# Modulation tiles multiplied in pairs, and the Hyena filters' two directions on the two halves of the array rows

## The chip, the core and the metric

The kernel runs on one NeuronCore of a Trainium2 chip. The metric is the device time of one execution in microseconds; a comparison is made between medians of runs on the same chip. One core has TensorE (PE; its weight loads are shown as PEld), VectorE (DVE), ScalarE (ACT), GpSimd (POOL) and SyncE (SP), which here only issues transfers, and 16 DMA engines. TensorE has two clock levels, 1.2 and 2.4 GHz; the profile shows the granted one as a share of the higher.

## What is computed

One inference step of a two-layer hybrid backbone, for a prompt of 128 tokens and a latent grid of 128 tokens with shared weights, in fp32. The parts that matter here:

```python
mod = silu(c) @ w_mod[l] + b_mod[l]          # 2048 -> 6 x 2048, for c_ctx and c; w_mod[l] is 100 MB
sh1, sc1, g1, sh2, sc2, g2 = split(mod, 6)
h = rms_norm(x, ln_mix) * (1 + sc1) + sh1
u_hy, u_gla, u_mla = split(h @ w_in)         # three mixers read the same h
x = x + g1 * (concat(hyena(u_hy), gla(u_gla), mla(u_mla)) @ w_out)
h = rms_norm(x, ln_ffn) * (1 + sc2) + sh2
x = x + g2 * ((silu(gate) * up) @ w_ffn_out) # gate, up = split(h @ w_ffn_in)

# hyena filters, the same for both token groups, once per layer
h = sin(freq[0] * (z @ w1 + b1))             # z: 128 x 33, w1: 33 x 64
h = sin(freq[1] * (h @ w2 + b2))             # w2: 64 x 64
k = (h @ w3) * decay                         # w3: 64 x (2 directions x 2 orders x 512 channels)
```

## The kernel before, in words

Both token groups lie side by side as 256 columns. The large products (`gemm_steps`, matmuls on line 343, tiles `pg`) split weights and activations into a high and a low fp32r part and run three matmuls for each block; for each k tile `weights` loads a tile `w` (five buffers), ScalarE writes `wh`, VectorE writes `wl`.

The modulation of a layer has six parts of 2048 columns. For layer 0 the first two are made in the prologue by `mod_first` (line 207, tiles of 256 columns and six buffers). Of the others, some run on VectorE beside the feed-forward part (`mod_dve`), and five run on TensorE (`mod_pe`, line 242): parts 2, 4 and 3 of layer 0 and parts 3 and 4 of layer 1, beside the three mixers and the output projection. For one part, `mod_pe` goes over 16 k tiles of 128 x 2048 fp32 (1 MB each, tag `mw` of the pool `mp`, which has **two** buffers). Each tile takes four matmuls: the stationary operand is the 128 x 32 piece `sc` of the conditioning vectors, the moving one a 128 x 512 view of the tile, and the four write the four 32-row strips of one PSUM bank `mps`, so they sit side by side in the four column groups of the array. A plain fp32 matmul stands in the profile as two records, so one tile is eight records of line 242.

`mod_pe` is a generator. `mod_tick(w)` moves it on by `rate` x w steps: `gemm_steps` ticks once for each k tile (weight: columns / 1024), `mla` with weight 10 for each pair of heads, `gla` and `hyena` with weight 14 for each token group; the rate is 0.36 in layer 0 and 0.2 in layer 1. So a tick of 14 in layer 0 is five steps with nothing else written between them. A step of the old form loads the next tile and multiplies the one loaded before.

The order on each engine is not the order of the code: the framework's scheduler places an instruction when its inputs are ready by its own reckoning, earlier code first. `add_manual_dep(a, b, no_sync)` keeps a behind b in that order. All weight loads and modulation loads are issued by SP, in order, and a load whose buffer is still in use holds back those behind it. The xs, constants, rows and filter weights are issued from ACT's queue.

`hyena_filters(pool, l)` runs in the prologue of layer 0 for both layers, between the first gemms: two small layers with a sine (lines 558 to 572), then for each of two orders and two directions one matmul with 64 rows of contraction (line 580) times `decay`, and the transform matrices (lines 585 to 589). The results go to DRAM and are read back by `hyena`. The bias and frequency rows come in through `rows2`, which line 516 transposes into `v2T`.

Of the kernel before, what the change touches and what calls it, by code (L numbers as in the profile page):

```python
# [17 lines left out]
KT = D // 128  # L18
# [9 lines left out]


MSTEP = 3  # L30
AHEAD = 4
FQ = 1
SPLIT = (4, 4, 4, 4)
# [69 lines left out]
def tile_backbone(ctx, tc, T, O):  # L103
# [52 lines left out]
            table["users"].append(r.ins.name)  # L156
        return r

    mm = nc.tensor.matmul

    def px(shape):
        return ps_x.tile(shape, F32, tag="x", name="px")
# [26 lines left out]
    def quads(w):  # L189
        return w.rearrange("p (k q j) -> p q k j", q=4, j=32)  # L190
# [39 lines left out]
    def mod_load(l, m, kt, pool):  # L230
        w = pool.tile([128, D], F32, tag="mw", name="mw")
        nc.sync.dma_start(w, T["w_mod"][l, kt * 128:(kt + 1) * 128, m * D:(m + 1) * D])
        return w

    def mod_pe(l, m, pool):
        ps = ps_m.tile([128, 512], F32, tag="mod", name="mps")
        nxt = mod_load(l, m, 0, pool)
        for kt in range(KT):
            w, nxt = nxt, mod_load(l, m, kt + 1, pool) if kt + 1 < KT else None
            wv = quads(w)  # L240
            for q in range(4):
                mm(ps[32 * q:32 * q + 32, :], sc[:, kt], wv[:, q], start=(kt == 0), stop=(kt == KT - 1))  # L242
            yield
        mod_finish(l, m, ps)
        yield

# [219 lines left out]
    with PR("px0") as pool:  # L466
        rows = pool.tile([128, 128], F32, name="rows")
        nc.sync.dma_start(rows[0:16], r128(T["c_ctx"], 16))
        nc.sync.dma_start(rows[16:32], r128(T["c"][0], 16))
        nc.scalar.dma_start(ident, T["mats"][:, 0])  # L470
        p = px([128, 128])
        nc.tensor.transpose(p[:, :32], rows[:32, :], ident[:32, :32])
        nc.vector.memset(sc, 0.0)
        act(sc[:, :, 0:2], p[:, 0:32].rearrange("p (g k) -> p k g", g=2), AF.Silu)

        at = 32
        for nm in ("ln_mix", "ln_ffn"):
            for l in range(DEPTH):
                nc.scalar.dma_start(rows[at:at + 16], r128(T[nm][l], 16))
                at += 16  # L480
        nc.scalar.dma_start(rows[at:at + 16], r128(T["ln_final"], 16))
        at += 16
        for nm, n in (("mla_q_norm", 3), ("mla_kv_norm", 2), ("gla_norm", 1)):
            for l in range(DEPTH):
                nc.scalar.dma_start(rows[at:at + n], r128(T[nm][l], n))
                at += n
        p = px([128, 128])
        nc.tensor.transpose(p[:, :at], rows[:at, :], ident[:at, :at])
        nc.vector.tensor_copy(out=vT[:, 32:at], in_=p[:, 32:at])

        for l in range(DEPTH):
            rb = pool.tile([128, 128], F32, tag="rb", name="rb")[:96]
            nc.scalar.dma_start(rb, r128(T["b_mod"][l], 96))
            p = px([128, 96])
            nc.tensor.transpose(p, rb, ident[:96, :96])
            nc.vector.tensor_copy(out=bT[:, l].rearrange("p m k -> p (m k)"), in_=p)

        for _ in mod_first(0, SPLIT[0], mp0, AHEAD):
            pass

        rows2 = pool.tile([128, 128], F32, tag="rb", name="rows2")
        nc.vector.memset(rows2, 0.0)
        at = 0
        for l in range(DEPTH):
            nc.scalar.dma_start(rows2[at:at + 36], T["hy_conv_w"][l].rearrange("i (r c) -> (i r) c", c=128))
            at += 36
        for l in range(DEPTH):
            nc.scalar.dma_start(rows2[at:at + 12], r128(T["hy_conv_b"][l], 12))
            at += 12
        for l in range(DEPTH):  # L510
            nc.scalar.dma_start(rows2[at:at + 1, :64], T["hy_filt_b1"][l:l + 1])
            nc.scalar.dma_start(rows2[at + 1:at + 2, :64], T["hy_filt_b2"][l:l + 1])
            nc.scalar.dma_start(rows2[at + 2:at + 4, :64], T["hy_filt_freq"][l])
            at += 4
        p = px([128, 128])
        nc.tensor.transpose(p[:, :at], rows2[:at, :], ident[:at, :at])
        nc.vector.tensor_copy(out=v2T, in_=p[:, :at])

        for half in range(2):
            xs = []  # L520
            for nm in ("x_prompt", "x_sample"):
                xt = pool.tile([128, D // 2], F32, tag="xin", name="xin", bufs=4)
                nc.scalar.dma_start(xt, T[nm][0, :, half * 1024:half * 1024 + 1024])
                xs.append(xt)
            for k4 in range(2):
                for g in range(2):
                    p = px([128, 4, 128])
                    for j in range(4):
                        k = 4 * k4 + j
                        nc.tensor.transpose(p[:, j], xs[g][:, 128 * k:128 * k + 128], ident)  # L530
                    k = 8 * half + 4 * k4
                    dst = xT[:, k:k + 4, 128 * g:128 * g + 128]
                    if g:
                        act(dst, p)
                    else:
                        nc.vector.tensor_copy(out=dst, in_=p)
        ss = SquareSum(pool)
        for k in range(0, KT, 2):
            ss.add(k, on_pe=(k == KT - 2), last=(k == KT - 2))
        rsq(rstd, ss.ps, ss.acc[:, 0:256])  # L540


    def hyena_filters(pool, l):
        w1 = pool.tile([33, 64], F32, tag="fw1", name="fw1")
        w2 = pool.tile([64, 64], F32, tag="fw2", name="fw2")
        zt = pool.tile([33, 128], F32, tag="fzt", name="fzt")
        skip = pool.tile([1, 1024], F32, tag="fsk", name="fsk")
        dec = pool.tile([128, HC], F32, tag="fdec", name="fdec")
        nc.scalar.dma_start(zt, T["zt"])
        nc.scalar.dma_start(w1, T["hy_filt_w1"][l])  # L550
        nc.scalar.dma_start(w2, T["hy_filt_w2"][l])
        nc.scalar.dma_start(dec, T["decay"])
        nc.scalar.dma_start(skip, T["hy_skip"][l:l + 1].rearrange("a o c -> a (o c)"))
        col = V2_F + 4 * l
        src, wgt = zt, w1
        for i in range(2):
            p = px([64, 128])
            mm(p, wgt, src, start=True, stop=True)
            b, f = v2T[:64, col + i:col + i + 1], v2T[:64, col + 2 + i:col + 3 + i]
            y = pool.tile([64, 128], F32, tag="fy", name="fy", bufs=2)  # L560
            k = pool.tile([64, 128], F32, tag="fk", name="fk")
            r = pool.tile([64, 128], F32, tag="fr", name="fr")
            ts(y, p, b, ALU.add, f, ALU.mult)
            ts(k, y, 1.0 / (2 * PI), ALU.mult)
            ts(k, k, 12582912.0, ALU.add)
            ts(k, k, 12582912.0, ALU.subtract)
            stt(r, k, -6.28125, y, ALU.mult, ALU.add)
            stt(r, k, -0.0019350051879882812, r, ALU.mult, ALU.add)
            stt(r, k, -3.019915981956753e-07, r, ALU.mult, ALU.add)
            ts(r, r, -3.1415925, ALU.max, 3.1415925, ALU.min)  # L570
            act(y, r, AF.Sin)
            src, wgt = y, w2
        for o in range(2):
            kt = {}
            for d in range(2):
                p = px([128, HC])
                c0 = (2 * d + o) * HC
                w3 = pool.tile([64, HC], F32, tag="fw3", name="fw3", bufs=2)
                nc.scalar.dma_start(w3, T["hy_filt_w3"][l, :, c0:c0 + HC])
                mm(p, src, w3, start=True, stop=True)  # L580
                kt[d, o] = pool.tile([128, HC], F32, tag=f"fkt{d}", name="fkt")
                tt(kt[d, o], p, dec, ALU.mult)
            tt(kt[0, o][0:1], kt[0, o][0:1], skip[:, o * HC:(o + 1) * HC], ALU.add)
            pr = px([128, HC])
            mm(pr, mats[:, M_FC], kt[0, o], start=True, stop=False)
            mm(pr, mats[:, M_BC], kt[1, o], start=False, stop=True)
            pi = px([128, HC])
            mm(pi, mats[:, M_FS], kt[0, o], start=True, stop=False)
            mm(pi, mats[:, M_BS], kt[1, o], start=False, stop=True)
            ks = pool.tile([128, 3, HC], F32, tag="fks", name="fks")  # L590
            act(ks[:, 0], pr)
            act(ks[:, 2], pr)
            nc.vector.tensor_copy(out=ks[:, 1], in_=pi)
            nc.vector.tensor_copy(out=ks[0:1, 2], in_=pi[0:1])
            nc.vector.memset(ks[0:1, 1], 0.0)
            nc.sync.dma_start(kspec[l][:, o], ks)
# [616 lines left out]
```

## Time and profile before

| what | value |
|---|---|
| median of 3 runs | 2512.07 us (2506.38 to 2512.3) |
| the profiled execution | 2512.27 us, its span 2510.5 us |
| PE busy | 2445.6 us (97%) |
| DVE busy | 1693.8 us (67%) |
| ACT busy | 1032.3 us (41%) |
| mean DMA rate | 239 GB/s, 601.21 MB |
| mean granted TensorE clock | 0.993 |

Times in rows are microseconds from the start of the span. A row of the timeline has start, length, engine, line, operation, output<-inputs, shape and the number of records merged in it; in brackets stands how long the engine had been idle before it, and what ended that. TensorE's matmuls are pipelined: the length of one is longer than the distance to the next, so what one costs is read from the distances between starts. A row of a table by stretches has the stretch, its length, the busy time (and number of records) of PE, PEld, DVE, ACT and POOL, the granted clock, the busy share of the DMA engines and GB/s. In a list of waits: waiter <- what it waited for, total us, times, longest. SPq and ACTq rows are transfers being issued.

### The profile page before, as it was taken

Reading aid. Unit: us, or ns where it says so; the run is one execution under the profiler, and the core shown is the slowest. Engines: PE = TensorE matmul, PEld = TensorE weight load, DVE = VectorE, ACT = ScalarE, POOL = GpSimd, SP = SyncE. Lnnn points to the kernel's source line nnn. Section 1 sums busy time; section 2 is a strip of 40 time slices with the busy share of each in tenths; the row PEclk is TensorE's granted clock in tenths of the full one; section 3 lists DMA queues with packets and bytes.
Section 4 is the critical chain, followed back from the end, with each engine's and each line's share of the span. In section 5 each row is a group of like instructions: output and inputs, shape, how many; then the busy total and the mean of one; then the engine's idle time right before and its main releaser. Section 6 shows DMA issues by size and latency. Waiting matters only on the chain.

```text
span 2510.5 us, 47020 instructions
## 1 busy us (share of the span) xinstructions
PE 2445.6 (97%) x19621; PEld 2254.7 (90%) x19621; DVE 1693.8 (67%) x2399; ACT 1032.3 (41%) x1405; POOL 0.2 (0%) x4
## 2 busy tenths in 40 slices
PE   6999999999999999999999999999999999999998
PEld 3567777999999999999998887899999999999998
DVE  2665555887879968988878556588684545454455
ACT  2334342454433333434446444335444334433443
POOL 0000000000000000000000000000000000000000
PEclk9999999999999999999999999999999999999998
DMA  8988888767768768777866667686765566555662
GB/s 291 332 297 306 292 298 301 282 221 250 264 224 292 284 228 302 238 258 258 288 227 190 214 240 243 218 298 215 252 234 178 184 185 185 177 186 166 184 204 93
DMA packets 167305, 601.21 MB, mean 239 GB/s; under 512 B 18576, under 2 KB 24882, under 8 KB 146612
## 3 DMA queue, kind: packets, MB, share of 16 engines
q1 hardware_dynamic: 164104, 592.27, 70.4%
q10 hardware_dynamic: 2988, 5.93, 0.7%
q8 instruction: 154, 2.52, 0.4%
q14 instruction: 59, 0.48, 0.1%
HBM read 592.03 MB, written 6.09 MB: 238 GB/s over the span
## 4 chain that ended last, share of the span: by engine, by line
PE 92%; DMA 4%; DVE 2%; ACT 1%; issue 0%; SPq 0%; DVEq 0%; ACTq 0%
PE pg L343 80%; DMA mw<-in_w_mod_dram 4%; PE mps L242 3%; PE px L862 2%; PE mps L207 1%; PE px L922 0%; PE px L426 0%; DVE macc L259 0%; PE px L268 0%; PE px L580 0%; PE px L623 0%; PE px L767 0%; DVE wl L126 0%; PE px L625 0%; PE px L914 0%
## 5 line engine op out<-in xcount | busy, mean ns | idle before, releaser
L126 DVE TENSOR_TENSOR wl<-w,wh 128x1024 fp32r<-128x1024 f32 (+3 forms) x816 | 872.2, 1086 | 547.5 <-ACT wh L153 543.2
L153 ACT ACTIVATE wh<-w 128x1024 fp32r<-128x1024 f32 (+3 forms) x816 | 767.8, 950 | 1140.3 <-PE pg L343 971.0
L343 PE MATMUL pg<-hh,wh 128*128 128x256 f32 x3648 | 1038.8, 286 | 9.9 <-ACT hh L153 9.1
L343 PE MATMUL pg<-hl,wh 128*128 128x256 f32 x3648 | 1035.0, 284 | 0.0
L343 PE MATMUL pg<-hh,wl 128*128 128x256 f32 x3648 | 1032.0, 284 | 2.7 <-DVE wl L126 2.7
L343 PEld LDWEIGHTS pg<-hh,wh 128*128 128x128 f32 x3648 | 688.8, 189 | 46.3 <-issue 26.5
L343 PEld LDWEIGHTS pg<-hl,wh 128*128 128x128 f32 x3648 | 691.4, 190 | 10.6 <-issue 9.1
L343 PEld LDWEIGHTS pg<-hh,wl 128*128 128x128 f32 x3648 | 689.8, 189 | 11.8 <-issue 7.2
L343 PE MATMUL pg<-al,wh 128*128 128x256 f32 x1408 | 396.8, 282 | 0.0
L343 PE MATMUL pg<-ah,wl 128*128 128x256 f32 x1408 | 395.0, 281 | 0.0
L343 PE MATMUL pg<-ah,wh 128*128 128x256 f32 x1408 | 395.0, 282 | 0.0
L259 DVE SCALAR_TENSOR_TENSOR macc<-mw,sc,macc 128x1024 f32<-128x1024 f32 x300 | 370.8, 1280 | 6.6 <-DMA mw<-in_w_mod_dram 6.6
L343 PEld LDWEIGHTS pg<-ah,wh 128*128 128x128 f32 x1408 | 264.6, 188 | 1.7 <-issue 1.7
L343 PEld LDWEIGHTS pg<-ah,wl 128*128 128x128 f32 x1408 | 265.6, 189 | 0.1
L343 PEld LDWEIGHTS pg<-al,wh 128*128 128x128 f32 x1408 | 265.5, 189 | 0.1
L242 PE MATMUL mps<-mw,sc 128*32 128x512 f32 x640 | 88.8, 604 | 10.4 <-DMA mw<-in_w_mod_dram 10.4
L131 DVE SCALAR_TENSOR_TENSOR xT<-pg,modv,xT 128x128 f32<-128x128 f32 x256 | 69.6, 343 | 24.0 <-PE pg L343 24.0
L343 PE MATMUL pg<-ymh,wh 128*128 128x256 f32 x256 | 72.4, 286 | 0.6 <-DVE xT L131 0.6
L343 PE MATMUL pg<-yml,wh 128*128 128x256 f32 x256 | 72.2, 283 | 0.0
L343 PE MATMUL pg<-ymh,wl 128*128 128x256 f32 x256 | 71.6, 283 | 0.0
L207 PE MATMUL mps<-mw,sc 128*32 128x256 f32 x512 | 45.2, 441 | 14.1 <-DMA mw<-in_w_mod_dram 14.1
L343 PEld LDWEIGHTS pg<-ymh,wh 128*128 128x128 f32 x256 | 48.8, 192 | 5.3 <-issue 5.0
(299 smaller groups left out, 1879.2 us busy)
## 6 DMA issues: line engine op xcount, KB each, us to landing
mw<-in_w_mod_dram SPq DMA_DIRECT2D x160, 1024.0 KB
w<-in_w_ffn_in_dram SPq DMA_DIRECT2D x256, 512.0 KB
w<-in_w_ffn_out_dram SPq DMA_DIRECT2D x176, 512.0 KB
w<-in_w_ffn_in_dram SPq DMA_DIRECT2D x128, 384.0 KB
mw<-in_w_mod_dram SPq DMA_DIRECT2D x64, 512.0 KB
w<-in_w_in_dram SPq DMA_DIRECT2D x64, 512.0 KB
w<-in_w_out_dram SPq DMA_DIRECT2D x64, 512.0 KB
w<-in_w_in_dram SPq DMA_DIRECT2D x64, 256.0 KB
```

The source lines that it names most:

```text
L126: r = nc.vector.tensor_tensor(out=out, in0=a, in1=b, op=op)
L131: r = nc.vector.scalar_tensor_tensor(out=out, in0=a, scalar=s, in1=b, op0=op0, op1=op1)
L153: r = nc.scalar.activation(out=out, in_=a, func=func, **k)
L207: mm(ps[32 * q:32 * q + 32, :], sc[:, kt], wv[:, q], start=(kt == 0), stop=(kt == KT - 1))
L242: mm(ps[32 * q:32 * q + 32, :], sc[:, kt], wv[:, q], start=(kt == 0), stop=(kt == KT - 1))
L259: r = nc.vector.scalar_tensor_tensor(out=acc[:, i, cs], in0=w[:, cs], scalar=c, in1=acc[:, i, cs], op0=ALU.mult, op1=ALU.add)
L343: mm(o, lt, rh, start=(ti == 0 and i == 0 and j == 0), stop=(ti == nt - 1 and i == len(ps) - 1 and j == 2))
L862: mm(o, a, b, start=(st and i == 0 and j == 0), stop=(en and i == len(steps) - 1 and j == 2))
```

## The change

1. `mod_pe` takes its tiles two at a time. One step loads both tiles of a pair, the next multiplies both, eight matmuls in a row, the tile loaded second first. `start` is now on tile 1 and `stop` on tile 14. The number of buffers stays two.
2. After such a pair the next `BURST` = 24 matmuls of the code that go through `mm` are tied behind the pair's last one, in order only. (Because `mm` is now a function, those matmuls all show line 164.)
3. In `hyena_filters` w1 and w2 are loaded twice side by side, so that the two sine layers give the same 64 rows twice, in partitions 0 to 63 and 64 to 127. The weights of the two directions lie in the two halves of one tile, and their two matmuls, each of 64 rows, are written one behind the other, into two PSUM banks.
4. For that, the bias and frequency rows are loaded twice into `rows2`.

```diff
+BURST = 24
...
-    mm = nc.tensor.matmul
+    burst = {"last": None, "left": 0}
+
+    def mm(*args, **kw):
+
+        r = nc.tensor.matmul(*args, **kw)
+        if burst["left"]:
+            burst["left"] -= 1
+            tc.add_manual_dep(r.ins, burst["last"], no_sync, reason="order")
+        return r
...
     def mod_pe(l, m, pool):
         ps = ps_m.tile([128, 512], F32, tag="mod", name="mps")
-        nxt = mod_load(l, m, 0, pool)
-        for kt in range(KT):
-            w, nxt = nxt, mod_load(l, m, kt + 1, pool) if kt + 1 < KT else None
-            wv = quads(w)
-            for q in range(4):
-                mm(ps[32 * q:32 * q + 32, :], sc[:, kt], wv[:, q], start=(kt == 0), stop=(kt == KT - 1))
+        for k0 in range(0, KT, 2):
+            ws = [mod_load(l, m, kt, pool) for kt in (k0, k0 + 1)]
             yield
+            burst["left"] = 0
+            for kt, w in ((k0 + 1, ws[1]), (k0, ws[0])):
+                wv = quads(w)
+                for q in range(4):
+                    r = mm(ps[32 * q:32 * q + 32, :], sc[:, kt], wv[:, q], start=(kt == 1), stop=(kt == KT - 2))
+            burst.update(last=r.ins.name, left=BURST)
+            if k0 + 2 < KT:
+                yield
         mod_finish(l, m, ps)
         yield
...
         for l in range(DEPTH):
-            nc.scalar.dma_start(rows2[at:at + 1, :64], T["hy_filt_b1"][l:l + 1])
-            nc.scalar.dma_start(rows2[at + 1:at + 2, :64], T["hy_filt_b2"][l:l + 1])
-            nc.scalar.dma_start(rows2[at + 2:at + 4, :64], T["hy_filt_freq"][l])
+            for h in (slice(0, 64), slice(64, 128)):
+                nc.scalar.dma_start(rows2[at:at + 1, h], T["hy_filt_b1"][l:l + 1])
+                nc.scalar.dma_start(rows2[at + 1:at + 2, h], T["hy_filt_b2"][l:l + 1])
+                nc.scalar.dma_start(rows2[at + 2:at + 4, h], T["hy_filt_freq"][l])
...
-        nc.scalar.dma_start(w1, T["hy_filt_w1"][l])
-        nc.scalar.dma_start(w2, T["hy_filt_w2"][l])
+        for i in range(2):
+            nc.scalar.dma_start(w1[:, i], T["hy_filt_w1"][l])
+            nc.scalar.dma_start(w2[:, i], T["hy_filt_w2"][l])
...
-            p = px([64, 128])
-            mm(p, wgt, src, start=True, stop=True)
+            p = px([128, 128])
+            mm(p, wgt.rearrange("p a c -> p (a c)"), src[0:wgt.shape[0]], start=True, stop=True)
...
+            w3 = pool.tile([128, HC], F32, tag="fw3", name="fw3", bufs=2)
             for d in range(2):
-                p = px([128, HC])
                 c0 = (2 * d + o) * HC
-                w3 = pool.tile([64, HC], F32, tag="fw3", name="fw3", bufs=2)
-                nc.scalar.dma_start(w3, T["hy_filt_w3"][l, :, c0:c0 + HC])
-                mm(p, src, w3, start=True, stop=True)
+                nc.scalar.dma_start(w3[64 * d:64 * d + 64], T["hy_filt_w3"][l, :, c0:c0 + HC])
+            ps = [px([128, HC]) for _ in range(2)]
+            for d in range(2):
+                r = slice(64 * d, 64 * d + 64)
+                mm(ps[d], src[r], w3[r], start=True, stop=True)
+            for d in range(2):
                 kt[d, o] = pool.tile([128, HC], F32, tag=f"fkt{d}", name="fkt")
-                tt(kt[d, o], p, dec, ALU.mult)
+                tt(kt[d, o], ps[d], dec, ALU.mult)
```

**TensorE at the second token group of gated linear attention, layer 0.** `mps` is the modulation's PSUM bank, `mw` a modulation tile, `pg` and `wh`/`wl` belong to the Hyena gemm that fills in, `px<-wa,afab` is the block's first own matmul. Before:

```order
L343 MATMUL pg_2660<-hh_88,wl_3043 128x256
L242 MATMUL mps_2764<-mw_2927,sc_93 32x512 x4
L242 MATMUL mps_2764<-mw_3100,sc_93 32x512 x4
L672 MATMUL px_3136<-wa_2648,afab_354 128x512
L343 MATMUL pg_2657<-hh_88,wh_3072 128x256
L343 MATMUL pg_2657<-hl_89,wh_3072 128x256
```

After:

```order
L164 MATMUL pg_2662<-hh_88,wl_3051 128x256
L164 MATMUL mps_2770<-mw_2939,sc_93 32x512 x4
L164 MATMUL mps_2770<-mw_2937,sc_93 32x512 x4
L164 MATMUL mps_2770<-mw_3118,sc_93 32x512 x4
L164 MATMUL mps_2770<-mw_3116,sc_93 32x512 x4
L164 MATMUL mps_2770<-mw_3130,sc_93 32x512 x4
L164 MATMUL mps_2770<-mw_3128,sc_93 32x512 x4
L164 MATMUL px_3144<-wa_2650,afab_360 128x512
L164 MATMUL pg_2659<-hh_88,wh_3080 128x256
```

Before, two tiles stand together, and the next five (`mw_3106` to `mw_3130`) follow singly, with 8 to 30 other rows between each two. Now three pairs stand in a row, and the block's first matmul behind all of them.

**SP's queue at the same place**: the loads of those tiles, among weight loads `w`. Before:

```order
L305 DMA w_3572<-in_w_in_dram 128x512 x2
L232 DMA mw_3106<-in_w_mod_dram 128x2048
L232 DMA mw_3112<-in_w_mod_dram 128x2048
L232 DMA mw_3118<-in_w_mod_dram 128x2048
L232 DMA mw_3124<-in_w_mod_dram 128x2048
L232 DMA mw_3130<-in_w_mod_dram 128x2048
```

After:

```order
L318 DMA w_3588<-in_w_in_dram 128x512 x2
L241 DMA mw_3116<-in_w_mod_dram 128x2048
L241 DMA mw_3118<-in_w_mod_dram 128x2048
L318 DMA w_3623<-in_w_in_dram 128x512 x2
L241 DMA mw_3128<-in_w_mod_dram 128x2048
L241 DMA mw_3130<-in_w_mod_dram 128x2048
```

Before, a single tile's load waits for one buffer. Now a pair's two loads wait for the two buffers of the pair before, and weight loads stand between pairs.

**TensorE in the filters of layer 1** (`px<-fw3,fy`: one direction of one order; `mps<-mw0`: the prologue's modulation), after the change:

```order
L164 MATMUL px_1568<-fw3_1565,fy_1553 128x512
L164 MATMUL mps_1219<-mw0_1346,sc_93 32x256 x4
L164 MATMUL px_1569<-fw3_1565,fy_1553 128x512
L164 MATMUL mps_1219<-mw0_1359,sc_93 32x256 x4
L164 MATMUL px_1577<-fkt_1572,mats_79 128x512
```

The two directions (`px_1568`, `px_1569`) have a modulation group between them; of the four such pairs in the two layers one stands without anything between.

## Rows read from the trace of the kernel before

**Rows 1.** Page, part 4: the chain that ended last, shares by engine, by line.
```profile
PE 92%; DMA 4%; DVE 2%; ACT 1%; issue 0%; SPq 0%; DVEq 0%; ACTq 0%
PE pg L343 80%; DMA mw<-in_w_mod_dram 4%; PE mps L242 3%; PE px L862 2%; PE mps L207 1%; PE px L922 0%; PE px L426 0%; DVE macc L259 0%; PE px L268 0%; PE px L580 0%; PE px L623 0%; PE px L767 0%; DVE wl L126 0%; PE px L625 0%; PE px L914 0%
```

**Rows 2.** Table by stretches: the two stretches in which `mod_pe` runs.
```profile
190.00:464.00 274.00, 265.64 (x2013) 202.39 (x2016) 157.34 (x287) 106.92 (x180) 0.00 (x0) 1.00 0.84 298
1321.00:1690.00 369.00, 364.59 (x2742) 310.41 (x2743) 242.28 (x445) 162.58 (x283) 0.00 (x0) 0.99 0.68 231
```

**Rows 3.** List of TensorE's waits: the modulation matmuls of line 242.
```profile
PE mps L242 <- DMA mw<-in_w_mod_dram: 10.4, 8, 3.7
```

**Rows 4.** Timeline of TensorE: one modulation tile between weight matmuls.
```profile
398.09 0.28 PE L343 MATMUL pg<-hl,wh 128*128 128x256 f32 x1
398.21 0.28 PE L343 MATMUL pg<-hh,wl 128*128 128x256 f32 x1
398.41 1.07 PE L242 MATMUL mps<-mw,sc 128*32 128x512 f32 x8
399.41 0.38 PE L343 MATMUL pg<-hh,wh 128*128 128x256 f32 x1
```

**Rows 5.** Timeline of TensorE: two modulation tiles in a row.
```profile
281.27 0.28 PE L343 MATMUL pg<-hh,wl 128*128 128x256 f32 x1
281.48 1.92 PE L242 MATMUL mps<-mw,sc 128*32 128x512 f32 x16
283.33 0.39 PE L343 MATMUL pg<-hh,wh 128*128 128x256 f32 x1
```

**Rows 6.** Timeline of SP and TensorE: the first modulation load and its use.
```profile
1.64 8.40 SPq L196 DMA_DIRECT2D mw<-in_w_mod_dram  x7
...
5.85 1.08 PE L207 MATMUL mps<-mw,sc 128*32 128x256 f32 x8 [2.50 <-DMA mw<-in_w_mod_dram]
```

**Rows 7.** Table by stretches: the fullest stretch of the prologue.
```profile
98.00:121.00 23.00, 21.06 (x177) 12.26 (x175) 10.03 (x33) 4.49 (x12) 0.00 (x0) 0.94 1.03 389
```

**Rows 8.** Timeline of SP and TensorE: loads behind the tiles of rows 5.
```profile
282.73 1.08 SPq L232 DMA_DIRECT2D mw<-in_w_mod_dram  x2
...
290.26 1.06 PE L242 MATMUL mps<-mw,sc 128*32 128x512 f32 x8 [1.23 <-DMA mw<-in_w_mod_dram]
```

**Rows 9.** Timeline of TensorE: MLA, behind a double modulation group.
```profile
216.53 0.39 PE L343 MATMUL pg<-hh,wl 128*128 128x256 f32 x1
...
220.36 1.57 PE L922 MATMUL px<-pt,v 128*128 128x128 f32 x12 [0.29 <-DVE pt L918]
221.69 0.36 PE L862 MATMUL px<-cqh,un 128*128 128x256 f32 x1
```

**Rows 10.** Timeline of TensorE: filter matmuls (64 rows); MLA scores (128, 64 rows).
```profile
73.03 1.12 PE L580 MATMUL px<-fw,fy 64*128 64x512 f32 x2
...
80.58 1.98 PE L580 MATMUL px<-fw,fy 64*128 64x512 f32 x4
...
213.08 0.38 PE L890 MATMUL px<-kn,qn 128*128 128x128 f32 x2
...
213.82 0.49 PE L894 MATMUL px<-krT,qr 64*128 64x128 f32 x4
```

**Rows 11.** Timeline and table by stretches: the start of layer 1.
```profile
1320.40 0.98 ACT L153 ACTIVATE hh<-nt,modv 128x128 fp32r<-128x128 f32 x3 [1.80 <-DVE nt L131]
1321.33 1.06 PE L242 MATMUL mps<-mw,sc 128*32 128x512 f32 x1 [3.69 <-DMA mw<-in_w_mod_dram]
...
1321.30:1325.00 3.70, 3.67 (x10) 2.00 (x11) 3.70 (x15) 1.88 (x6) 0.00 (x0) 0.50 0.97 367
1325.00:1330.00 5.00, 5.00 (x37) 5.00 (x36) 2.37 (x8) 2.65 (x8) 0.00 (x0) 0.82 0.09 29
```

**Rows 12.** Timeline of TensorE: transposes of x around a late modulation load.
```profile
31.70 0.64 PE L530 MATMUL px<-ident,xin 128*128 128x128 f32 x2
...
33.64 2.18 PE L530 MATMUL px<-ident,xin 128*128 128x128 f32 x9
37.90 1.08 PE L207 MATMUL mps<-mw,sc 128*32 128x256 f32 x8 [2.08 <-DMA mw<-in_w_mod_dram]
```

More of the change, by code (lines that the diff above doesn't have):

```diff
@@ L543, in hyena_filters @@
     def hyena_filters(pool, l):
-        w1 = pool.tile([33, 64], F32, tag="fw1", name="fw1")
-        w2 = pool.tile([64, 64], F32, tag="fw2", name="fw2")
+        w1 = pool.tile([33, 2, 64], F32, tag="fw1", name="fw1")
+        w2 = pool.tile([64, 2, 64], F32, tag="fw2", name="fw2")
         zt = pool.tile([33, 128], F32, tag="fzt", name="fzt")
@@ L556, in hyena_filters @@
         for i in range(2):
-            p = px([64, 128])
-            mm(p, wgt, src, start=True, stop=True)
[L559 to L562, printed above, removed]
+            p = px([128, 128])
+            mm(p, wgt.rearrange("p a c -> p (a c)"), src[0:wgt.shape[0]], start=True, stop=True)
+            b, f = v2T[:, col + i:col + i + 1], v2T[:, col + 2 + i:col + 3 + i]
+            y = pool.tile([128, 128], F32, tag="fy", name="fy", bufs=2)
+            k = pool.tile([128, 128], F32, tag="fk", name="fk")
+            r = pool.tile([128, 128], F32, tag="fr", name="fr")
             ts(y, p, b, ALU.add, f, ALU.mult)
```

## The prediction

> **What bounds the kernel now.** I read the page's chain of waits first: 92% of it is TensorE, and 80% of the span is the weight matmuls of line 343 [rows 1]. So work beside TensorE costs nothing, and an edit counts by what it adds to or takes from TensorE's queue, or by a wait there. Then the stretches in which `mod_pe` runs, 190 to 464 us in layer 0 and 1321 to 1690 us in layer 1: TensorE is busy 266 of 274 and 365 of 369 us, and in the first the DMA engines are busy 84% of the time at 298 GB/s [rows 2]. That stage is nearly full on both sides. Third, TensorE's own waits: for modulation loads on line 242 it lost 10.4 us in 8 waits [rows 3]. Merging and better hiding can win little; a new wait on TensorE costs its full length.
>
> **What holding pairs together saves.** One group of four 32-column matmuls stretches the step from one weight matmul to the next from 0.12 to 1.20 us, so it costs 1.08 us [rows 4]. Two groups in a row make it 2.06 us, cost 1.94 [rows 5]. So a run costs 0.22 us once and 0.86 per group; a group torn in two pays 0.86 twice. The old order has 73 runs of line 242 with 85 groups or parts (80 loads, five groups torn); the new one has 43 runs and 88 parts, because the tie only holds back the next 24 matmuls and others still slip in. 73 x 0.22 + 85 x 0.86 = 89.2 us against 43 x 0.22 + 88 x 0.86 = 85.1 us: **4.0 us saved**.
>
> **What it costs.** The pool `mp` has two buffers, and it keeps two. Before, one load was in flight while the other tile was multiplied, and a group that came late let later matmuls pass. Now a pair fills both buffers, the next pair's loads can start only when this pair's matmuls free them, and the 24 matmuls behind each pair wait with it. So between the end of one pair and the start of the next TensorE needs either other work or idle time, as long as 2 MB take to come.
>
> How long that is: at the start the first 0.5 MB is issued at 1.64 and used at 5.85 us [rows 6]. At the 389 GB/s of the fullest stretch [rows 7] 0.52 MB (512 KB) take 1.35 us, which leaves 4.21 - 1.35 = 2.85 us that do not depend on size; 2.1 MB take 5.4 us, so 8.25 us from the first issue, which can come some 0.75 us before the pair's end, when its first half has freed a buffer: 7.5 us. The second look is at 282.73 us, where two loads go out together, behind weights, after a double group that ends at 283.33; the first is in use at 290.26, 6.9 us after that end [rows 5, 8]. I take **7.2 us**, between the two. Bounds: 4.6 us if nothing but the transfer counts (5.4 - 0.75), and 9.5 us with 0.8 MB of weights ahead in the queue, since SP issues in order and a few weight loads stand between the pairs.
>
> The Trainium skill, "DMA: Bandwidth & Descriptors", section "Bandwidth", says that for loads from HBM the HBM side binds at about 358 GB/s. The trace's 389 GB/s is above that; by the page each pair would take 0.5 us longer, and the sum would be 8 us higher.
>
> Now the new order. Five pairs follow another pair with **no** row between: one in the first and two in the second gated-linear-attention block of layer 0, one in each of layer 1. There `mod_tick(14)` takes five steps at once. 5 x 7.2 = **36.0 us**. Eleven more pairs have less than 7.2 us of work between, adding up the rows at the spacings that the trace shows (0.12 us for 256 columns [rows 4] and twice that for 512, 0.86 for a plain fp32 matmul of 512 [rows 10], 0.22 for one of 128 [rows 9]): 6.8, 5.2, 5.2, 4.6, 4.0, 3.5, 6.6, 5.1, 2.8, 5.0 and 5.3 us. The two of 5.2 lie in MLA, from the pair behind the scores to the end of the products with v; I take them from the trace, where that stretch lasts from 216.53 to 221.69, the softmax wait included [rows 9]. Together they lack 79.2 - 54.1 = **25.1 us**. The other 24 pairs have cover.
>
> **The clock.** After the one wait of 3.69 us for a modulation load, TensorE's granted clock is 0.50 (1.2 of 2.4 GHz) from 1321.3 to 1325.0 us and 0.82 over the next 5 us [rows 11]: 3.7 + 1.8 = 5.5 us at half speed, 2.75 us lost. Shorter waits, as the 1.23 us at 290 [rows 8], left it full. Seven of my waits reach 3.69 us (five of 7.2, and those with covers of 3.5 and 2.8): 19.25 us. One of them makes the cover behind it last longer, which hides that pair's 2.6 us: **16.6 us**. Bounds: nothing, and 33 us if a pair takes 9.5 us, when thirteen waits are that long.
>
> **What goes away.** The 10.4 us of old waits are replaced, except the 3.69 at 1321.33: there TensorE would have stood until the new layer's `hh` was there anyway, the activation that writes it begins at 1320.40 [rows 11]. I count 7.0 us.
>
> **Filters.** Two matmuls on the two halves of the rows need 0.49 us for four records where one on all rows needs 0.38 for two [rows 10]: they do run side by side. A neighbouring pair thus saves one, 1.98 - 1.12 = 0.86 us [rows 10]. But in the new order one pair of four is adjacent; in two a modulation group of another shape stands between, in the last one eight weight matmuls. **0.9 us**. The Trainium skill, "TensorEngine Tiling (Array Packing)", section "Theoretical Speedup", promises up to 2x at a contraction of 64; for all four pairs that would be 3.4 us. The wider tiles of the sine chain have the same elements per partition: nothing. Four more weight loads and six more row loads go to ACT's queue; ScalarE has 1% of the chain [rows 1], so they cost nothing by themselves.
>
> **The start.** With those six, the transpose of `rows2` moves behind another modulation group, the one for which TensorE waits until 37.90 us, and with it eleven transposes of x that ran before it [rows 12]: 11 x 0.24 = 2.6 us later. But from 98 to 121 us the loads are the limit (share 1.03) and TensorE is idle 1.9 of 23 us [rows 7], which takes most of that up. Between 0 and 2.6 I take **1.0 us** more.
>
> **Sum.** 36.0 + 25.1 + 16.6 + 1.0 - 4.0 - 7.0 - 0.9 = +66.8 us. The profiled execution took 2512.27 us, 0.2 above the median of the runs shown. **2579 us.** With 6.5 us per pair the same working gives 2566, with 9.5 us (the pair with 7.3 us of cover then waits too) 2634.
>
> **The rivals.**
> - Loads in time, so faster. If 2 MB came within the cover everywhere, the old waits would go whole: -10.4 - 4.0 - 0.9 + 1.0, 2498 us. It decides at the cover: 7.2 us for every pair, where five have none. For it: TensorE now waits only 10.4 us in all. Against it: those loads are spread singly over the stage. 4%.
> - Only the five bare pairs wait, because the shorter covers hide vector work on which TensorE has to wait anyway, and the clock holds: +36.0 - 10.9 = 25, 2537 us. For it: the hyena and softmax chains do wait on VectorE. Against: the 3.69 us wait did lower the clock. 15%.
> - The loads are held up behind blocked weight loads in SP's queue, 9.5 us per pair, as bounded above: 47.5 + 52.6 + 33.1 - 10.9 = +122, 2634 us. For it: of the two loads that went out at 282.73 behind weights the first alone needed 7.5 us [rows 8]. 12%.
> - No change: the stage is bound by its transfers, and idle moments on TensorE only move. For it: 84% DMA share. Against: TensorE is busy 97% there. 3%.
>
> **How the numbers follow.** My forecast has 64%; 2% is left for what I don't see. The range, 2535 to 2625, takes in the second rival and stops short of the third's full price. Faster by over 0.3% (7.5 us, what a measurement here can tell) has the first rival's 4%, no change 3%, slower 93%.
>
> **What would show it.** In the changed profile the waits of the `mps` matmuls beside the mixers for modulation loads (they show line 164 now) should be some 60 us, five of them near 7 us in the two attention blocks, with the granted clock at 0.5 behind them; a pair (16 records) should cost 1.94 us where it does not wait. DMA share from 190 to 464 us should fall. I am wrong if the waits stay under 20 us, or if a 7 us wait leaves the clock full; or if the time comes back elsewhere, which would show as TensorE being idle less in the later parts of these stages than now.

## The result, and the profile after

| kernel | median us | ratio to before, 95% interval |
|---|---|---|
| before, on the same chip | 2509.23 (4 runs, with the three of the section on the time before) | 1 |
| the change | 2612.30 (4 runs, 2607.57 to 2615.54) | 1.0409 [1.0394, 1.0425] |

The change is slower by 4.1%, 103 us. The forecast was 2579, the range 2535 to 2625. The profiled execution took 2611.59 us with a span of 2609.8; against the profiled one of before that is 99.3 us, and the sums below are made against that.

The page of the change, part 1 (busy time, share of the span, instructions), all engines:

```profile
PE 2474.3 (95%) x19621; PEld 2266.6 (87%) x19621; DVE 1693.8 (65%) x2399; ACT 1032.8 (40%) x1405; POOL 0.2 (0%) x4
```

TensorE has the same number of matmuls as before (19621), yet it is idle 2609.8 - 2474.3 = 135.5 us where it was 2510.5 - 2445.6 = 64.9, and busy 28.7 us longer. So there are two losses, one in waits and one in work that takes longer. TensorE's waits in the change, whole span:

```profile
PE mps L164 <- DMA mw<-in_w_mod_dram: 77.5, 36, 9.5
PE pg L164 <- ACT hh L154: 11.7, 4, 3.5
PE px L164 <- DVE yre L127: 6.9, 3, 2.4
...
PE px L1033 <- DVE u L132: 4.4, 4, 1.6
PE px L932 <- DVE e L137: 3.7, 5, 1.5
```

Since all matmuls through `mm` show line 164, the first row holds the prologue too. The same list cut to the parts with the mixers and the output projection, in which `mod_pe` runs, 195 to 606 us in layer 0 and then 1370 to 1800 us in layer 1:

```profile
PE mps L164 <- DMA mw<-in_w_mod_dram: 35.2, 9, 9.5
...
PE mps L164 <- DMA mw<-in_w_mod_dram: 19.0, 5, 8.6
```

So 54.2 us of waits for modulation loads stand where [rows 3] had 10.4. Table by stretches, of the change (columns as in [rows 2]: length, busy time and records of PE, PEld, DVE, ACT, POOL, granted clock, DMA share, GB/s):

```profile
190.00:530.00 340.00, 289.01 (x2047) 212.64 (x2046) 162.54 (x298) 107.53 (x182) 0.00 (x0) 0.91 0.68 242
1370.00:1740.00 370.00, 342.29 (x2467) 283.88 (x2467) 209.10 (x426) 151.94 (x283) 0.00 (x0) 0.94 0.59 200
```

Where layer 0's stretch was full on both sides [rows 2], now the DMA share is 0.68 instead of 0.84 and the clock 0.91 instead of 1.00: TensorE waits for loads and the DMA engines stand idle in turn, since each waits for the other. Timeline of TensorE in the second attention block of layer 0, of the change:

```profile
346.04 0.28 PE L164 MATMUL pg<-hh,wl 128*128 128x256 f32 x1
346.26 1.92 PE L164 MATMUL mps<-mw,sc 128*32 128x512 f32 x16
357.72 3.64 PE L164 MATMUL mps<-mw,sc 128*32 128x512 f32 x16 [9.54 <-DMA mw<-in_w_mod_dram]
368.42 3.64 PE L164 MATMUL mps<-mw,sc 128*32 128x512 f32 x16 [7.07 <-DMA mw<-in_w_mod_dram]
371.99 1.38 PE L164 MATMUL px<-wa,afab 33*128 33x512 f32 x2
```

These are two of the five pairs with no row between. The first pair takes 1.92 us as in [rows 5]; the two behind a wait take 3.64, at half clock, as in [rows 11]. Table by stretches, of the change, there:

```profile
360.00:370.00 10.00, 2.94 (x16) 0.40 (x12) 0.00 (x0) 0.00 (x0) 0.00 (x0) 0.50 0.60 211
```

The other three waits are 7.51, 8.42 and 8.58 us. SP's queue there, of the change:

```profile
346.39 0.80 SPq L318 DMA_DIRECT2D w<-in_w_in_dram  x2
347.39 1.19 SPq L241 DMA_DIRECT2D mw<-in_w_mod_dram  x2
348.67 1.76 SPq L318 DMA_DIRECT2D w<-in_w_in_dram  x2
359.71 12.74 SPq L241 DMA_DIRECT2D mw<-in_w_mod_dram  x4
```

The pair's loads go out at 347.39, while the pair before is multiplied, as the prediction had it (some 0.8 us ahead of its end at 348.2). Two weight loads are issued just ahead of them and two just behind, and that wait is 9.54; the next pair's loads have none beside them, and that wait is 7.07. The three others have one or two weight loads right behind them as well, at 7.51 to 8.58, so weights beside a pair go with a longer wait, but no run tries them apart.

Where the 99.3 us lie, by matching the same matmuls in both traces: the first 190 us 3.5, layer 0's mixers 62, layer 1's 34, the rest within a microsecond of nothing.

### The profile page after: what moved, and what is told of

The parts are those of the page before. It is cut to its first block, busy times and chain, and to the rows that moved or that the text cites. A ratio compares the mean times of both kernels' runs of the same rounds, so it can differ in the third digit from the quotient of the medians.

```text
span 2609.8 us, 47022 instructions
## 1 busy us (share of the span) xinstructions
PE 2474.3 (95%) x19621; PEld 2266.6 (87%) x19621; DVE 1693.8 (65%) x2399; ACT 1032.8 (40%) x1405; POOL 0.2 (0%) x4
## 5 line engine op out<-in xcount | busy, mean ns | idle before, releaser
L164 PE MATMUL mps<-mw,sc 128*32 128x512 f32 (+1 forms) x1152 | 148.3, 592 | 77.6 <-DMA mw<-in_w_mod_dram 77.5
L164 PEld LDWEIGHTS mps<-mw,sc 128*32 128x32 f32 x1152 | 32.5, 119 | 153.0 <-DMA mw<-in_w_mod_dram 86.0
```

The lines of the kernel that those rows point to most:

```text
L164: r = nc.tensor.matmul(*args, **kw)
```

## Experiments

Each was run beside the kernel before on the same chip. Ratios are given against that; 0.001 is 2.5 us. The kernel before took 2509 us on the chip of experiments 1 and 2 and 2513 to 2514 on those of the others, so kernels of different experiments are compared by their ratios.

**1. The tie taken away.** The whole change, except

```diff
-BURST = 24
+BURST = 0
```

> The change whole, with BURST = 0: pairs, but no matmul tied behind a pair. Theory A (the tie makes the waits): without it the order of TensorE has other work between any two pairs, by the spacings of the trace 5.6 to 9.7 us where the change has none, so no wait is above 3 us, the waits of mps beside the mixers fall from 54 us to under 12 us, the clock holds there, and the time is 2500 to 2520 us. Theory B (two buffers that a pair fills at once are enough, whatever stands behind it): every pair with little cover still waits some 3 to 8 us and the clock falls; over 2570 us.

2515.93 us, 1.0027 [1.0014, 1.0039]. TensorE's waits in the parts with `mod_pe` (195 to 540 us, then 1310 to 1700 us) of this kernel:

```profile
PE mps L164 <- DMA mw<-in_w_mod_dram: 4.7, 3, 2.1
...
PE mps L164 <- DMA mw<-in_w_mod_dram: 1.6, 2, 0.8
```

54.2 us of waits became 6.3, and the waits for `yre` are gone from the list. The pairs and the two buffers are the same; the order now has 5.6 us or more of other matmuls between any two pairs. Theory A holds, theory B falls: two buffers do for pairs, if the scheduler may put something between. The tie costs 1.0409 - 1.0027, 96 us.

**2. Filters alone, pairs alone, single tiles tied.** The old `mod_pe` with the new filters; the new `mod_pe` and tie with the old filters and rows; and the old `mod_pe` with this at its end:

```diff
-                mm(ps[32 * q:32 * q + 32, :], sc[:, kt], wv[:, q], start=(kt == 0), stop=(kt == KT - 1))
+                r = mm(ps[32 * q:32 * q + 32, :], sc[:, kt], wv[:, q], start=(kt == 0), stop=(kt == KT - 1))
+            burst.update(last=r.ins.name, left=BURST)
```

(`burst["left"] = 0` stands ahead of each tile's matmuls; the filters of this third kernel are the new ones.)

> Only the filters of the change; modulation tiles one by one as before. Both theories: the filters and the later start of the prologue cost little, the profile of the change shows the first 190 us longer by some 3.5 us for the same matmuls; 2509 to 2516 us. Rival: the filters' side of the change carries a good part of the 103 us (through the clock in the prologue, or matmuls that come out of place later): 2530 us or more.

> Only the pairs with their tie of 24; filters and rows as before. Theory A and B: the whole loss less some 3 us, 2605 to 2612 us, five bare waits of 7 to 10 us. Rival (the filters carry a good part): 2590 us or less.

> Tiles one by one as before, one loaded ahead, but the next 24 matmuls are tied behind each tile; filters as in the change. Theory A (the tie): the order again has tiles with no row between (in runs of four and six in layer 0, three in layer 1), of which the first two are there and each later one waits some 3.3 us (5.6 us for 1 MB and 1 us of matmuls, for two tiles in flight): 7 such waits, 23 us, with some 10 us of clock, 2530 to 2555 us. Theory B (pairs that fill both buffers): no more than before, 2505 to 2515 us.

| kernel | median us | ratio, 95% interval |
|---|---|---|
| filters alone | 2526.11 | 1.0071 [1.0055, 1.0087] |
| pairs alone | 2606.19 | 1.0378 [1.0359, 1.0398] |
| single tiles tied | 2564.96 | 1.0226 [1.0210, 1.0242] |

The pairs with their tie carry the loss, as expected. The filters cost 0.7%, 18 us alone, against some 3 expected: a miss, taken up in 4. On top of the pairs they cost 1.0409 - 1.0378, 8 us, which the intervals don't tell from 3. Single tiles tied lose 1.0226 - 1.0071, 39 us: the tie hurts the old form too, more than I expected (2530 to 2555). Their bare waits come in twos, since two loads are issued together. Timeline of TensorE, layer 0, of that kernel:

```profile
346.88 1.94 PE L164 MATMUL mps<-mw,sc 128*32 128x512 f32 x8 [4.54 <-DMA mw<-in_w_mod_dram]
349.41 1.93 PE L164 MATMUL mps<-mw,sc 128*32 128x512 f32 x8 [0.59 <-DMA mw<-in_w_mod_dram]
354.78 1.94 PE L164 MATMUL mps<-mw,sc 128*32 128x512 f32 x8 [3.44 <-DMA mw<-in_w_mod_dram]
```

So neither half alone gives the 96 us: the tie on single tiles costs 39, the pairs without it nothing (1.0027, where the filters alone have 1.0071).

**3. One pair per tick.** What is left of a tick waits for the next:

```diff
-            while st[2] >= 1.0:
-                st[2] -= 1.0
-                next(st[0], None)
+            for _ in range(2):
+                if st[2] >= 1.0:
+                    st[2] -= 1.0
+                    next(st[0], None)
```

> The change, but a tick runs at most two steps and keeps the rest for the next one, so that one tick of 14 cannot write two pairs. Theory (tick and tie together make the bare pairs): by the order two of five bare pairs stay, three shorter covers of 4.6 us come in their place; three waits of 8.2 us and their 3.5 us of clock go, some 8 us come back; 2578 to 2592 us. Rival (the tie alone, the tick changes only where the pairs stand): 2603 us or more.

2579.13 us, 1.0267 [1.0247, 1.0288], 36 us under the change: as expected. So the tick of five steps has a part in the bare pairs. But 1.0267 - 1.0027, 60 of the 96 us, stay with the tie alone: two bare pairs remain (waits of 7.00 and 7.01 us), and short covers bring others, the longest 6.25 us.

**4. The filters without extra loads.** From 2, with every doubled piece loaded by one transfer that reads its source twice:

```diff
-        for i in range(2):
-            nc.scalar.dma_start(w1[:, i], T["hy_filt_w1"][l])
-            nc.scalar.dma_start(w2[:, i], T["hy_filt_w2"][l])
+        nc.scalar.dma_start(w1, T["hy_filt_w1"][l].unsqueeze(1).to_broadcast([33, 2, 64]))
+        nc.scalar.dma_start(w2, T["hy_filt_w2"][l].unsqueeze(1).to_broadcast([64, 2, 64]))
```

and the rows in the same way.

> The filters alone again, but each doubled row and weight comes by one transfer whose source is read twice, so ScalarE's queue issues as many loads as before. Theory: the ten extra loads are what costs, they hold up ScalarE by some 4 us ahead of the copies of x, and the first weight matmul starts at 58 us where before it started at 53; then that start is back at 53 to 54 us and the time is 2510 to 2521 us. Rival: the filters' later and side-by-side matmuls cost, or the clock that falls beside them: 2523 to 2529 us as filters_alone.

2517.91 us, 1.0017 [1.0007, 1.0027]. So 0.0054, 14 of the filters' 18 us (9 to 18 by the intervals), went with the ten extra loads. The timeline of filters alone, transpose of `rows2` and first weight matmul:

```profile
38.04 0.44 PE L526 MATMUL px<-ident,rows 104*128 104x104 f32 x1
...
58.24 0.62 PE L164 MATMUL pg<-hh,wh 128*128 128x256 f32 x3 [1.65 <-ACT hh L154]
```

and of this kernel:

```profile
33.71 0.41 PE L527 MATMUL px<-ident,rows 104*128 104x104 f32 x1 [2.24 <-DMA rows<-in_hy_filt_b_dram]
...
53.80 0.62 PE L164 MATMUL pg<-hh,wh 128*128 128x256 f32 x3 [2.07 <-ACT hh L154]
```

The start moves by 4.4 us, but that isn't all of it. TensorE's waits for modulation loads in the first 197 us, of filters alone and then of this kernel:

```profile
PE mps L164 <- DMA mw<-in_w_mod_dram: 21.1, 19, 4.6
...
PE mps L164 <- DMA mw<-in_w_mod_dram: 13.9, 13, 3.4
```

The kernel before has 14.1 there. So with the extra loads TensorE also waits 7 us longer for modulation tiles in the prologue. The two profiled executions, 2523.45 and 2519.45 us, differ by 4.0 us alone, so no trace shows all 14.

The 4 us that remain are a loss too, where I had forecast a gain. Table by stretches, the prologue of this kernel and of the kernel before:

```profile
0.00:197.00 197.00, 164.54 (x1144) 103.45 (x1145) 103.79 (x259) 61.73 (x133) 0.20 (x4) 0.95 0.86 299
```

```profile
0.00:190.00 190.00, 160.15 (x1140) 102.02 (x1141) 103.59 (x259) 61.42 (x132) 0.20 (x4) 0.97 0.89 307
```

The granted clock is lower. Added up over the stretches at half clock, TensorE's work in the prologue takes 9.3 us longer than at full clock, where in the kernel before it takes 4.7 longer. That has the size of the remaining loss; it was not tried by itself.

**5. Pairs without tie and without the new filters.** Experiment 1 with the old filters and rows.

> Pairs without the tie, filters and rows as before. If pairs as such gain what pairs_untied gained on filters_alone (2516 against 2526 us), this is faster than before: 2495 to 2503 us. Rival: that gain was only the filters' loss made good later, in a stage that had slack for it; then 2506 to 2512 us.

2507.70 us against 2513.49 of before beside it, 0.9973 [0.9962, 0.9983]. The expectation was written for a before of 2509, for which this ratio gives 2502: faster than before, by 7 us. (The time as it stands, 2507.70, lies in the rival's range; on this chip, by the ratios, that range would begin at 2510.) So pairs as such seem to gain, but experiment 7 has a second look at it that shows less.

**6. The waits filled with work.** Ahead of each of the five bare pairs:

```diff
+            bare = (l, m, k0) in ((0, 4, 2), (0, 4, 8), (0, 4, 10), (1, 3, 12), (1, 4, 0))
+            for i in range(8 if bare else 0):
+                for q in range(4):
+                    nc.tensor.matmul(ps[32 * q:32 * q + 32, :], zero, mats[:, 0:4].rearrange("p a c -> p (a c)"),
+                                     start=(k0 == 0 and i == 0), stop=False)
```

(`zero`, a tile of 128 x 32 zeros, is allocated ahead of `sel`; the pair that begins a sum leaves `start` to the zeros.)

> The change, with 32 matmuls by a stationary operand of zeros (6.9 us at full clock) written into the same bank ahead of each of the five pairs that have no row between them and the pair before. They fill the wait with work and make no transfer earlier. Theory: the waits cost a second time through the clock, some 17 us at half clock behind these five; with the waits filled it stays full there and the time is 2590 to 2601 us, with under 3 us left of each of the five waits. Rival: the lower clock has another cause or costs nothing, because the work behind it waits for loads anyway; then 2606 to 2616 us, or more.

2587.53 us, 1.0297 [1.0283, 1.0311]. Timeline of TensorE in the block shown above, of this kernel:

```profile
346.87 1.92 PE L164 MATMUL mps<-mw,sc 128*32 128x512 f32 x16
348.62 7.05 PE L255 MATMUL mps<-mats,zero 128*32 128x512 f32 x64
358.64 1.92 PE L164 MATMUL mps<-mw,sc 128*32 128x512 f32 x16 [2.98 <-DMA mw<-in_w_mod_dram]
360.38 7.05 PE L255 MATMUL mps<-mats,zero 128*32 128x512 f32 x64
367.95 1.92 PE L164 MATMUL mps<-mw,sc 128*32 128x512 f32 x16 [0.52 <-DMA mw<-in_w_mod_dram]
```

The pairs come no earlier after one another (6.9 us of zeros and 0.5 to 3.0 us of wait are the old waits), but they take 1.92 us, not 3.64: the clock holds. The gain, 1.0409 - 1.0297 or 28 us, was more than theory and rival allowed for, and the trace showed why: in this kernel the weight matmuls came about a nanosecond sooner also in the feed-forward parts (118.2 for 119.7 ns in layer 0's, 119.0 for 119.5 from 1900 to 2400 us). The tile of zeros moves the tiles allocated behind it in memory. So it needed a control.

**7. The unused tile alone.** In the change, in the kernel before, and in 5:

```diff
+    pad = base.tile([128, 32], F32, name="pad")
+    nc.vector.memset(pad, 0.0)
     sel = base.tile([128, 2, 32], F32, name="sel")
```

> The change with the same unused tile: the control for zero_fill. Theory L: some 10 to 16 us under the change, 2596 to 2603 us, so that the zeros themselves gave only the rest, some 10 to 15 us. Rival: the time of the change, 2607 to 2616 us, and the zeros gave all of the 25 us.

> The kernel before, with one unused tile of 128 x 32 fp32 allocated ahead of sel, as zero_fill has it; nothing else, the order of the instructions is the same. Theory L (place in memory): in zero_fill each weight matmul came 1.2 ns sooner in all stages (118.3 ns from start to start for 119.5) because the 128 bytes move the tiles behind them; then this kernel gains as much on its 16000 such matmuls, 2492 to 2502 us. Rival: that was a matter of that run or of the zeros; then 2506 to 2513 us at 119.5 ns.

> Pairs without the tie, filters as before (untied_old_filters), with the same unused tile. Theory L: both gains, 2485 to 2496 us. Rival: 2500 to 2508 us as without it.

| kernel | median us | ratio, 95% interval |
|---|---|---|
| the change, with the tile | 2596.44 | 1.0334 [1.0316, 1.0353] |
| before, with the tile | 2493.68 | 0.9928 [0.9916, 0.9941] |
| pairs without tie, old filters, with the tile | 2491.25 | 0.9914 [0.9899, 0.9930] |

The unused tile gives 0.6 to 0.75% in all three, theory L. Against its control, the zeros of 6 gave 1.0334 - 1.0297, 9 us (3 to 15 by the intervals); that is what the clock behind the five waits costs. The third kernel has the lowest median of the study, but between it and the second the intervals overlap: with the tile in both, pairs gain 0.0014, where experiment 5 had 0.0027. That pairs as such gain at all is so not shown beyond doubt; the forecast's 4.0 us lie between the two.

**8. Half the bytes.**

```diff
-            ws = [mod_load(l, m, kt, pool) for kt in (k0, k0 + 1)]
+            ws = []
+            for kt in (k0, k0 + 1):
+                w = pool.tile([128, D], F32, tag="mw", name="mw")
+                nc.sync.dma_start(w[:, 0:1024], T["w_mod"][l, kt * 128:(kt + 1) * 128, m * D:m * D + 1024])
...
-                    r = mm(ps[32 * q:32 * q + 32, :], sc[:, kt], wv[:, q], start=(kt == 1), stop=(kt == KT - 2))
+                    r = mm(ps[32 * q:32 * q + 32, :], sc[:, kt], w[:, 512 * (q % 2):512 * (q % 2) + 512], start=(kt == 1), stop=(kt == KT - 2))
```

> The change, but only the first half of each row of a modulation tile is loaded, and the matmuls read that half twice (so the modulation computed on TensorE is another one). Theory: a bare pair waits for its transfer, 2.85 us and then the bytes; with 1 MB in place of 2 the five waits fall from 8.2 us to 5 to 6 us, most waits behind short covers vanish, the clock falls less; 2560 to 2585 us. Rival: the loads are held up in SP's queue or by their fixed time, size does not matter; the waits stay at 7 us or more and the time above 2595 us.

2577.17 us, 1.0257 [1.0241, 1.0273], as expected. Timeline of TensorE at the same place, of this kernel:

```profile
342.68 3.64 PE L164 MATMUL mps<-mw,sc 128*32 128x512 f32 x16 [6.24 <-DMA mw<-in_w_mod_dram]
351.04 3.64 PE L164 MATMUL mps<-mw,sc 128*32 128x512 f32 x16 [4.72 <-DMA mw<-in_w_mod_dram]
```

The five waits are 5.24, 6.24, 4.72, 4.72 and 6.01 us, 5.4 on average, where 2 MB gave 41.1 / 5 = 8.2. So, as an estimate, 1.05 MB take 2.8 us (370 GB/s, with weights beside them), and 2.6 us behind the end of the pair before do not depend on size.

The Trainium skill, "SBUF — State Buffer", section "The DMA setup-cost knee", fits a load as 2 us and the bytes at 436 GB/s. By that, an estimate, 1.05 MB less would save 2.4 us; the runs show 2.8 in company of weight loads. The fixed part is longer here than the page's 2 us: 2.6 us behind the pair's end, to which comes the time, some 0.8 us, by which the load was issued ahead of it.

## Why the prediction was right, and where it was short

The direction, the main mechanism and the range held; the size was short, 2579 for 2612, or +66.8 for the +99 that the terms below add up to. The terms of the prediction, against what the two profiles give:

| term | forecast us | measured us |
|---|---|---|
| five bare pairs | +36.0 | +41.1 |
| short covers | +25.1 | +13.1 |
| new waits for VectorE and ScalarE | 0 | +19.3 |
| old waits | -7.0 | -6.9 |
| clock | +16.6 | +31 |
| merging | -4.0 | -2 |
| filters and start | +0.1 | +3.5 |
| sum | +66.8 | +99 |

The waits are sums of TensorE's idle times in the parts with `mod_pe`. The clock is half of the time in which TensorE worked at half clock, 34.0 us there less 2.7 before. Filters and start are the shift of the first 190 us. Merging is what is left, so it takes up the errors of all the others.

**Five bare pairs: right, by 1 us each too short.** 7.2 us was taken, 8.2 measured. By experiment 8, half of that lies in the fixed time (2.6 us behind the pair's end for 2.85 - 0.75 = 2.1), 0.3 in the rate (370 GB/s for the 389 of the best stretch [rows 7]), and the rest in my taking 7.2 where the first estimate had 7.5. The third rival (9.5 us, weights in SP's queue) has its price in one of the five, the one of 9.54; the others, 7.07 to 8.58, lie below it.

**Why they are bare: half right.** The prediction put it down to the tick of five steps. Experiment 1 shows that without the tie no pair is bare, experiment 3 that with the tie and no such tick 60 of 96 us stay, and experiment 2 that the tie harms even single tiles. So the tie is the main cause, and the tick adds to it. The 24 matmuls behind a pair are the next of the code, among them the mixer's own chain, and not only filling work.

**Short covers: the right work, the wrong wait.** 25.1 us were forecast as waits for loads; 13.1 came so, but 19.3 us of new waits for VectorE and ScalarE came too. Timeline of TensorE in the Hyena mixer of layer 0, of the change:

```profile
413.11 0.72 PE L1033 MATMUL px<-ident,u 128*128 128x128 f32 x4 [1.57 <-DVE u L132]
...
415.55 3.64 PE L164 MATMUL mps<-mw,sc 128*32 128x512 f32 x16 [0.88 <-DMA mw<-in_w_mod_dram]
419.12 1.71 PE L164 MATMUL px<-vt,mats 128*128 128x512 f32 x2
423.00 1.31 PE L164 MATMUL px<-yre,mats 128*128 128x512 f32 x2 [2.17 <-DVE yre L127]
```

The transform matmuls (`vt,mats`) stand behind the pair, so their result reaches VectorE later, and TensorE waits for VectorE's product with nothing between. The second rival had seen that short covers hide vector work, and drew from it that nothing is lost; the loss only changed its name. Without the tie the wait for `yre` is absent.

**The clock: mis-sized, by 14 us; with the covers and the new waits taken together (32.4 us for 25.1), the largest error.** Each wait of 3.69 us or more was charged 2.75 us, and shorter ones nothing, as the 1.23 us at 290 us had left the clock full. Experiment 6 shows the mechanism and a net price: five filled waits give back 9 us, and the time lost at work by the granted clock falls from 30.0 us in its control to 19.8. Of the 34.0 us, by the same sum, 17.2 lie in the stretches at half clock about the five bare pairs, where 13.8 were forecast, and 16.8 in others, where 2.9 were. What I missed is mostly those others. Table by stretches, of the change, in the Hyena mixer of the rows just shown:

```profile
413.50:420.30 6.80, 5.73 (x23) 1.38 (x20) 0.89 (x2) 1.09 (x2) 0.00 (x0) 0.50 1.03 375
423.80:430.60 6.80, 5.95 (x17) 1.25 (x19) 1.98 (x3) 0.00 (x0) 0.00 (x0) 0.50 0.25 104
```

No wait there was above 2.2 us, but several followed each other; outside the five, no wait beside the mixers reached 3.69 us (the longest 3.56). So charging nothing for waits shorter than 3.69 us was the step of the clock term that failed. The trace of before had shown as much. Timeline and table by stretches, of the kernel before:

```profile
544.20 0.73 PE L343 MATMUL pg<-hh,wh 128*128 128x256 f32 x4 [3.50 <-ACT hh L153]
...
545.10:548.50 3.40, 3.40 (x18) 3.40 (x18) 3.40 (x13) 1.39 (x4) 0.00 (x0) 0.51 0.02 5
```

A wait of 3.50 us had half clock behind it (0.51 in this stretch, 0.50 from 1729.6 to 1733.0 us behind the same wait in layer 1).

**Merging: right in kind.** Where a pair does not wait it costs what [rows 5] shows. Timeline of TensorE, of the change:

```profile
443.04 0.28 PE L164 MATMUL pg<-hh,wl 128*128 128x256 f32 x1
443.26 1.92 PE L164 MATMUL mps<-mw,sc 128*32 128x512 f32 x16
445.11 0.38 PE L164 MATMUL pg<-hh,wh 128*128 128x256 f32 x1
```

2.07 us from weight matmul to weight matmul. Untied pairs are 7 us faster than before in experiment 5, and 0.0014 or 3.5 us, within the noise, with the unused tile in both (experiment 7); the forecast's 4.0 fits either.

**Old waits: right.** 10.4 less the 3.69 that the prediction excepted is 6.7, not its 7.0. The 3.69 us at the start of layer 1 [rows 11] went, and TensorE waits 3.5 us for `hh` there instead.

**Filters: the saving right, its place too small to matter, one step wrong.** The adjacent pair of layer 0, timeline of TensorE of the change:

```profile
117.64 1.13 PE L164 MATMUL px<-fw,fy 64*128 64x512 f32 x4
```

Four records in 1.13 us where [rows 10] has 1.98: 0.85 saved, 0.86 forecast. The Trainium skill's page "TensorEngine Tiling (Array Packing)", section "Theoretical Speedup", is borne out to 1.75 of its 2x, and only for the one adjacent pair. The step that failed is "ScalarE has 1% of the chain [rows 1], so they cost nothing by themselves": experiment 4 puts 14 us on them. ScalarE issues these loads itself, at 0.23 to 0.27 us each, ahead of the copies of x on which the first gemm waits. In the change that gemm begins at 57.66 us, where it began at 53.17. The lower clock in the prologue, 0.94 in the first 190 us of the change for 0.97 before, stood in no term at all. A share of the chain over the span says nothing of a stage in which that engine is on the path.

**The rivals.** Loads in time: excluded, 54.2 us of waits. No change: excluded. Only the five waits with a full clock (2537): its two conditions both failed. Loads held up (2634): its time is nearer to the 2612 measured than my 2579, but that is in part luck. Of its terms the clock's 33.1 us fits (31 measured), while the bare pairs took 41.1 of its 47.5 us, and covers and new waits together 32.4 of its 52.6.

## What to carry to other kernels

A group that fills all its buffers needs other work behind it for as long as its next loads take; whatever takes the scheduler's freedom to put it there (here an order-only tie) costs that time. Charge a wait to the engine's queue and not to the named cause: what is held back also comes late to the other engines, and here both long waits and runs of short ones cost once more through TensorE's clock. When an edit adds a tile, give the control the same tile, since its place in memory can be worth more than the edit.

## What was not expected of the hardware

An unused tile of 128 bytes per partition, allocated ahead of the weight tiles, with the same order of instructions, made the kernel 0.6 to 0.75% faster in three kernels. Table by stretches, the kernel before, in two stretches where TensorE does little but weight matmuls:

```profile
600.00:700.00 100.00, 100.00 (x835) 100.00 (x835) 70.59 (x65) 41.69 (x43) 0.00 (x0) 1.00 0.75 249
1900.00:2400.00 500.00, 500.00 (x4176) 499.94 (x4175) 247.74 (x282) 203.92 (x218) 0.00 (x0) 1.00 0.61 181
```

and with the unused tile:

```profile
600.00:700.00 100.00, 100.00 (x847) 99.99 (x846) 70.75 (x64) 41.72 (x43) 0.00 (x0) 1.00 0.73 252
1900.00:2400.00 500.00, 500.00 (x4204) 499.88 (x4203) 248.81 (x283) 205.58 (x220) 0.00 (x0) 1.00 0.59 184
```

At the full clock 847 matmuls fit where 835 did, 118.1 ns each for 119.8; in the second stretch it is less, 118.9 for 119.7. The order of TensorE's instructions in the two traces is the same throughout. By the order of allocation, the tiles behind the unused one, `w`, `wh`, `wl` and `mw` among them, move by these 128 bytes. That it is their addresses is argued from this; what in them does it was not tried.
